# Retention's sample outputs in a decoder layer: the product of state and query columns moved from TensorE to ScalarE and VectorE, with TensorE summing one block a sample

## The chip, the cores and the metric

The kernel runs on one core of a Trainium2 chip. The metric is the device time of one execution in microseconds (us). Three executions were timed before the change; their median is 2566.97 us. The engines are named as in the profile: PE is TensorE (PEld its weight loads), DVE is VectorE, ACT is ScalarE, POOL is GpSimd, and SP is the engine whose queue issues nearly all transfers. Each of them works through its own list of instructions in order; an instruction that has to wait holds up all that stand behind it in its list.

## The reference

One decoder layer runs for two groups: a prompt of 16 + 256 tokens, and 8 samples that each have one new token and a state of earlier tokens. The layer is a feed-forward block, a mixer and a second feed-forward block. The mixer has two branches, and the change is in the retention branch: 8 heads with keys of 256 features and values of 256. For a sample it comes down to

```python
def retention_chunk(S, q, k, v):
    ...
    o = jnp.einsum('bhij,bhjv->bhiv', inner, v) + jnp.einsum('bhid,bhdv->bhiv', q_dec, S)
    ...
    S_new = jnp.exp(lg * C)[:, None, None].astype(S.dtype) * S + jnp.einsum('bhjd,bhjv->bhdv', k_dec, v)
    return S_new.astype(S.dtype), o
```

With one token a sample this is the same as: the new state is S_new = gamma * S + k v^T (256 x 256 a sample and head), and the output is o = S_new^T q, a row of 256. S_new is itself an output of the kernel (state_ret_sample), and o goes on through a normalisation, a gate and the output projection.

## The kernel before

Tokens stand in columns and features in the 128 partitions, so a vector of 256 features is two halves of 128 partitions each. All dense products (feed-forward blocks, the mixer's input projection, its output projection) are done by one loop, `dense` (L201 to L220): for each 128 x 128 block of weights there are three matmuls at L218, since a weight is split in two parts, `whi` and `wlo`, and so are the tokens (`xh`, `xl`). The weights come in units of eight blocks (512 KB). One unit takes these steps in `stream` (L170): a transfer into `raw` (L185, issued by SP), a copy to `whi` on ACT (L188), a subtraction that gives `wlo` on DVE (L189), and then 24 matmuls on PE. `raw`, `whi` and `wlo` have three buffers each. SP can issue the transfer of a unit only when DVE has made the `wlo` of the unit three before it, and ACT can make a `whi` only when PE has finished with the unit three before it.

The input projection (`project`) runs head after head, with the next head's columns in front of the previous head's gates. Between its steps of k, `pump` (L617) lets other work in: the mixers of the heads are generators (`mix_hg` for the other branch, `mix_ret` for retention), and `yield n` in them means that n pumps go by before the next piece is issued. On PE the order is as written; on the other engines the scheduler orders the work, and it gives the weight steps of `stream` high priority.

`mix_ret(u, q, k, v)` does retention for head u. What matters here of its sample part:

- Four tiles `sms[0]` to `sms[3]` (tag `smr`, four buffers that `ks` and `vs` use too) hold the states of the head: `sms[2 * e + c]` has half c of the key features for the four samples 4e to 4e + 3, as 128 partitions x 4 x 256.
- ACT scales a tile by gamma (L1192, four ACTIVATEs a head of 128 x 1024), and DVE adds key times value (L1198, sixteen instructions a head of 128 x 256, one for each sample and half). The result is the new state, in place.
- SP stores each tile to `out_srs` (L1202), four stores of 512 KB a head, here called S1 to S4: S1 and S2 are the halves 0 and 1 of e = 0, S3 and S4 those of e = 1.
- After more pumps, PE makes the outputs of the eight samples in the bank `pqr` (L1211): for each sample and half one matmul whose moving operand is the 128 x 256 state and whose stationary operand is 32 columns of `qdr`, a tile of zeros in which only the sample's own query column stands. So 16 matmuls a head go into four groups of 32 rows (`tile_position`), in which the sums run over halves and over e. `alone(qdr, q)` (L1133, helper L733) puts the query's columns in place on DVE, once a head.
- ACT copies `pqr` out (L1217), and `sample_columns` (L738) later turns the rows into columns of the head's output.

These matmuls only read the tiles, and a store only reads them too, so before the change neither waits for the other.

Of the kernel before, what the change touches and what calls it, by code (L numbers as in the profile page):

```python
# [13 lines left out]
AF = mybir.ActivationFunctionType  # L14
ALU = mybir.AluOpType
# [3 lines left out]
P = 128  # L19
# [4 lines left out]
NMETA, SEQ, NS = 16, 256, 8  # L24
# [27 lines left out]
ALONE = 4 * 32 + 1  # L52
# [76 lines left out]
def trunk(ctx: ExitStack, tc: tile.TileContext, A, O):  # L129
    nc = tc.nc  # L130
# [12 lines left out]
    def mx_bank(name):  # L143
        return ps_m.tile([P, 512], F32, tag="mx", name=name)
# [94 lines left out]
    def mul(out, a, b):  # L239
        nc.vector.tensor_tensor(out=out, in0=a, in1=b, op=ALU.mult)  # L240
# [306 lines left out]
    with tc.tile_pool(name="yp", bufs=1) as yp:  # L547
# [7 lines left out]
        with tc.tile_pool(name="mp", bufs=1) as mp:  # L555
# [7 lines left out]
            def tmp(name, shape=(P, T), bufs=1, dt=F32, tag=None):  # L563
                if name in rows:
                    rows[name] = rows[name][1:] + rows[name][:1]
                    return rp.tile(list(shape), dt, tag=rows[name][-1], name=name)
                return mp.tile(list(shape), dt, tag=tag or name, name=name, bufs=bufs)
# [19 lines left out]


            qdh = tmp("qdh", (P, 4, ALONE))
            qdr = tmp("qdr", (P, 4, ALONE))  # L590
            nc.gpsimd.memset(qdh, 0.0)
            nc.gpsimd.memset(qdr, 0.0)
            qdh_at = [qdh.rearrange("p a c -> p (a c)")[:, 256 * h :] for h in range(2)]
            qdr_at = [qdr.rearrange("p a c -> p (a c)")[:, 2 * ALONE * c :] for c in range(2)]
            vsm = tmp("vsm", (P, P))
            vt2 = tmp("vt2", (P, 2, P))
            scr2 = tmp("scr2", (P, NMETA))
# [50 lines left out]
            def evacuate(n, c0, c1, o0, o1, b0, b1):  # L648
# [33 lines left out]
                elif n == "v_r":  # L682
                    v = tmp("v", (P, 2, T))
                    nc.scalar.copy(v[:, 0, :], o0)
                    nc.scalar.copy(v[:, 1, :], o1)
                    start(mix_ret(c0 // 2, st["q_r"], st["k_r"], v), 24 if c0 == 2 else 3)
                elif n in ("g_r", "g_h"):
                    sg = tmp("gs", (P, TL), bufs=2)
                    t = tmp("gt", (P, TL), bufs=2)
                    nc.scalar.activation(sg, o0, AF.Sigmoid)  # L690
                    mul(t, sg, o0)
                    sa = tmp("gs", (P, TL), bufs=2)
                    nc.scalar.activation(sa, o1, AF.Sigmoid)
                    mul(t, t, sa)
                    u, e = divmod(c0, 2)
                    while u not in (done_r if n == "g_r" else done_h):
                        pump()
                    if n == "g_r":
                        y = tmp("y", (P, TL))
                        mul(y, t, on_r[u][:, e, :])  # L700
                        st["y"] = y
                    else:
                        y = st["y"]
                        nc.vector.scalar_tensor_tensor(
                            out=t, in0=t, scalar=ngt[:, c0 : c0 + 1], in1=on_h[u][:, e, :], op0=ALU.mult, op1=ALU.mult)

                        ys[c0] = y if c0 < EARLY else yp.tile([P, TL], F32, tag=f"y{c0}", name=f"y{c0}")
                        add(ys[c0], y, t)
                        if c0 < EARLY:
                            split(yh[c0], yl[c0], y)  # L710
# [22 lines left out]
            def alone(qd, q):  # L733
                nc.vector.tensor_copy(
                    qd[:, :, : 128 : 32].rearrange("p (c e) j -> p c e j", e=2),
                    q[:, :, SEQ:].rearrange("p c (e j) -> p c e j", e=2))
# [348 lines left out]
            def mix_ret(u, q, k, v):  # L1085
# [3 lines left out]
                calm = 2  # L1089
                sms = []  # L1090
# [13 lines left out]
                for c in range(2):  # L1104
# [22 lines left out]
                    for x, g, his, i, lo in todo:  # L1127
                        for hi in his:
                            nc.scalar.activation(hi, x, AF.Copy, scale=g)
                        nc.vector.scalar_tensor_tensor(  # L1130
                            out=lo, in0=x, scalar=g, in1=his[i].bitcast(F32), op0=ALU.mult, op1=ALU.subtract)
                    yield 2
                alone(qdr, q)  # L1133
                vts = [vt[:, 0], vt[:, 1], vs2]
                vrow = rows_out(vt2.rearrange("p c f -> p (c f)")[16:24, :], 256, "vr")

# [25 lines left out]
                for c in range(2):  # L1162
# [9 lines left out]
                    if c == 0:  # L1172
                        gams = [tmp("gam", (P, 1))]
                        nc.gpsimd.tensor_scalar(
                            out=gams[0], in0=so[:, 0:1], scalar1=GAMMA[u], scalar2=GAMMA[u], op0=ALU.min, op1=ALU.max)
# [13 lines left out]
                for e in range(2):  # L1189
# [3 lines left out]
                    for i in (2 * e, 2 * e + 1):  # L1193
                        for c in range(2):
                            for b in (2 * i, 2 * i + 1):
                                x, t = ss[c][:, b - 4 * e, :], LP + b
                                kk = late_k[:, c, b - 4 : b - 3] if e else k[:, c, t : t + 1]
                                nc.vector.scalar_tensor_tensor(  # L1198
                                    out=x, in0=vbs[i][:, b - 2 * i, :], scalar=kk, in1=x, op0=ALU.mult, op1=ALU.add)
# [1 line left out]
                    for c in range(2):  # L1201
                        nc.sync.dma_start(O["srs"][u, c, :, 4 * e : 4 * e + 4, :], ss[c])  # L1202
                    yield 1 if e else 10 if u == 0 else 6
                yield (11 if u == 0 else 15) + 2 * calm
                pq = mx_bank("pqr")
                scores(pq[:, 256:], 2)
                for e in range(2):
                    for c in range(2):
                        for j in range(4):
                            b = 4 * e + j  # L1210
                            nc.tensor.matmul(  # L1211
                                pq[32 * j : 32 * j + 32, :256], qdr_at[c][:, 32 * b : 32 * b + 32],
                                sms[2 * e + c][:, j, :], start=e + c == 0, stop=e + c == 2, tile_position=(0, 32 * j))
                mul(scr2[:NB2], pq[:NB2, 256 : 256 + NMETA], dt[:NB2, c2:])
                upper_upper_lower(sc2, scr2[:NB2])
                os = tmp("osr", (P, 256))
# [160 lines left out]
```

## Time and profile before

| | |
| --- | --- |
| time, median of 3 (lowest to highest) | 2566.97 us (2566.27 to 2568.13) |
| span of the profiled execution, first to last instruction | 2563.9 us |
| stretch in which `pqr` matmuls run (8 heads) | 859.8 to 1698.6 us |
| transfers of the core over the span | 536.26 MB, mean 209 GB/s |

The profile gives a span for the profiled execution, and no time of its own beside it; the median stands 3.07 us above that span, and this is taken for what lies around it. In the tables below, a row of a timeline has the start in us, the duration in us (of the whole row where several instructions are merged), the engine, the line, the operation, `out<-in` with the program's names, and the count; a bracket behind it tells how long the engine sat idle before it and what ended that. A row of a group has the count, then busy us and mean ns of one, then idle us before and what ended it. Matmuls in fp32 show as two records each, so the 16 matmuls of a head are 32 records. "SPq" is SP's queue of transfers, and the times in its rows are those of the issue, not of the transfer.

### The profile page before, as it was taken

How to read it: one execution, taken by the hardware profiler on the slowest of the kernel's cores; microseconds unless marked ns; L12 is line 12 of the kernel's file. 1: busy time of each engine (PE TensorE's matmuls, PEld its weight loads, DVE VectorE, ACT ScalarE, POOL GpSimd, SP SyncE). 2: the span in 40 equal slices, each digit the busy share in tenths (PEclk: the TensorE clock that was granted, in tenths of full speed). 3: DMA queues.
4: the chain of work that ended last, by engine and by line, in shares of the span. 5: the costliest groups of instructions: out<-in, count | busy, mean ns of one | idle time of the engine just before them, and what ended most of it. 6: DMA issues, size and time to landing. Idle time of an engine off the chain costs nothing.

```text
span 2563.9 us, 56275 instructions
## 1 busy us (share of the span) xinstructions
PE 2553.4 (100%) x23424; PEld 2534.4 (99%) x23424; DVE 1702.8 (66%) x2827; ACT 1392.2 (54%) x2186; POOL 57.0 (2%) x152
## 2 busy tenths in 40 slices
PE   9999999999999999999999999999999999999999
PEld 9999999999999999999999999999999999999998
DVE  6444544475569878777777777777885555556555
ACT  5444444444456767767676666675564444444443
POOL 0000000000000000000000000000000000000000
PEclk9999999999999999999999999999999999999999
DMA  7555555555555876767676767675556565565554
GB/s 244 183 187 183 187 182 184 186 182 186 184 201 180 287 265 232 264 214 260 212 264 215 259 223 255 224 239 188 196 190 197 194 197 195 194 196 195 195 195 149
DMA packets 156897, 536.26 MB, mean 209 GB/s; under 512 B 17952, under 2 KB 25952, under 8 KB 156640
## 3 DMA queue, kind: packets, MB, share of 16 engines
q1 hardware_dynamic: 156352, 532.37, 62.0%
q8 instruction: 183, 3.00, 0.5%
q14 instruction: 74, 0.61, 0.1%
q10 hardware_dynamic: 288, 0.29, 0.0%
HBM read 501.99 MB, written 30.61 MB: 208 GB/s over the span
## 4 chain that ended last, share of the span: by engine, by line
PE 96%; DVE 2%; ACT 0%; issue 0%; DMA 0%; SPq 0%; ACTq 0%; DVEq 0%
PE up L218 36%; PE dn L218 19%; PE pj_i_h L218 3%; PE pj_g_r L218 3%; PE pj_q_h L218 3%; PE pj_g_h L218 3%; PE pj_a_r L218 3%; PE pj_a_h L218 3%; PE pj_f L218 3%; PE pj_q_r L218 3%; PE pj_k_r L218 3%; PE wo L218 3%; PE pj_v_r L218 3%; DVE wlo L189 1%; PE pqr L1211 1%; PE psr L1168 0%
## 5 line engine op out<-in xcount | busy, mean ns | idle before, releaser
L189 DVE TENSOR_TENSOR wlo<-raw,whi 128x1024 fp32r<-128x1024 f32 (+1 forms) x869 | 1062.2, 1223 | 740.7 <-ACT whi L188 737.3
L188 ACT CAST whi<-raw 128x1024 fp32r<-128x1024 f32 (+1 forms) x870 | 905.7, 1042 | 909.2 <-PE up L218 411.0
L218 PE MATMUL up<-xh,whi 128*128 128x280 f32 (+1 forms) x2624 | 725.6, 280 | 0.6 <-ACT whi L188 0.6
L218 PE MATMUL up<-xh,wlo 128*128 128x280 f32 (+1 forms) x2624 | 725.8, 280 | 0.4 <-DVE wlo L189 0.3
L218 PE MATMUL up<-xl,whi 128*128 128x280 f32 (+1 forms) x2624 | 725.4, 279 | 0.0
L218 PEld LDWEIGHTS up<-xh,wlo 128*128 128x128 f32 x2624 | 492.6, 189 | 1.0 <-DVE wlo L189 1.0
L218 PEld LDWEIGHTS up<-xh,whi 128*128 128x128 f32 x2624 | 492.6, 189 | 0.8 <-ACT whi L188 0.8
L218 PEld LDWEIGHTS up<-xl,whi 128*128 128x128 f32 x2624 | 492.6, 189 | 0.0
L218 PE MATMUL dn<-hh,whi 128*128 128x280 f32 (+1 forms) x1376 | 384.7, 280 | 0.0
L218 PE MATMUL dn<-hh,wlo 128*128 128x280 f32 (+1 forms) x1376 | 384.3, 279 | 0.0
L218 PE MATMUL dn<-hl,whi 128*128 128x280 f32 (+1 forms) x1376 | 384.3, 279 | 0.0
L218 PEld LDWEIGHTS dn<-hh,whi 128*128 128x128 f32 x1376 | 260.1, 189 | 0.1
L218 PEld LDWEIGHTS dn<-hl,whi 128*128 128x128 f32 x1376 | 260.1, 189 | 0.1
L218 PEld LDWEIGHTS dn<-hh,wlo 128*128 128x128 f32 x1376 | 260.1, 189 | 0.0
L218 PE MATMUL pj_k_r<-xh,whi 128*128 128x280 f32 x256 | 74.2, 290 | 0.0
L218 PE MATMUL pj_g_r<-xh,whi 128*128 128x264 f32 x256 | 74.0, 289 | 0.0
L218 PE MATMUL pj_v_r<-xh,whi 128*128 128x280 f32 x256 | 73.8, 288 | 0.0
L218 PE MATMUL pj_v_r<-xh,wlo 128*128 128x280 f32 x256 | 72.4, 283 | 0.3 <-DVE wlo L189 0.3
L218 PE MATMUL pj_g_h<-xh,whi 128*128 128x264 f32 x256 | 72.7, 284 | 0.0
L218 PE MATMUL pj_k_r<-xh,wlo 128*128 128x280 f32 x256 | 72.4, 283 | 0.0
L218 PE MATMUL pj_v_r<-xl,whi 128*128 128x280 f32 x256 | 72.3, 283 | 0.0
L218 PE MATMUL pj_k_r<-xl,whi 128*128 128x280 f32 x256 | 72.3, 283 | 0.0
(421 smaller groups left out, 5263.4 us busy)
## 6 DMA issues: line engine op xcount, KB each, us to landing
raw<-in_w_up SPq DMA_DIRECT2D x343, 512.0 KB, 4.1
raw<-in_w_in SPq DMA_DIRECT2D x320, 512.0 KB, 4.3
raw<-in_w_dn SPq DMA_DIRECT2D x172, 512.0 KB, 3.5
smr<-in_sr SPq DMA_DIRECT2D x32, 512.0 KB, 5.0
out_srs<-smr SPq DMA_DIRECT2D x32, 512.0 KB, 6.7
raw<-in_w_out SPq DMA_DIRECT2D x32, 512.0 KB, 3.9
vbr<-vrd SPq DMA_DIRECT2D x32, 256.0 KB, 4.1
smh<-in_sg SPq DMA_DIRECT2D x16, 512.0 KB, 5.2
```

Source lines behind the costliest of these rows:

```text
L188: nc.scalar.copy(hi[:, j:jn, :], raw[:, j:jn, :])
L189: nc.vector.tensor_tensor(out=lo[:, j0:j1, :], in0=raw[:, j0:j1, :], in1=hi[:, j0:j1, :].bitcast(F32), op=ALU.subtract)
L218: nc.tensor.matmul(o, w, t, start=start, stop=stop)
L1211: nc.tensor.matmul(pq[32 * j : 32 * j + 32, :256], qdr_at[c][:, 32 * b : 32 * b + 32], sms[2 * e + c][:, j, :], start=e + c == 0, stop=e + ...
```

## The change

The product of state and query column leaves PE. A new tile `one` takes the place of `qdr`: zeros with a column of ones at the sample's place, set once for all heads. After the new state has been made and its stores have been issued, ACT multiplies half 0 of each sample's state by the query column's half 0, in place (eight ACTIVATEs of 128 x 256 a head), and DVE multiplies half 1 by the query's half 1 and adds what ACT made, in place (eight instructions of 128 x 256). PE then only has to sum over the 128 partitions: one matmul a sample with the ones, 8 a head where there were 16. `alone(qdr, q)` goes away. The single `yield` ahead of the matmuls is cut into pieces with the same sum, so that the two parts of four samples are issued some pumps ahead.

```diff
             qdh = tmp("qdh", (P, 4, ALONE))
-            qdr = tmp("qdr", (P, 4, ALONE))
+            one = tmp("one", (P, 2, ALONE))
             nc.gpsimd.memset(qdh, 0.0)
-            nc.gpsimd.memset(qdr, 0.0)
+            nc.gpsimd.memset(one, 0.0)
+            nc.gpsimd.memset(one[:, :, : 128 : 32], 1.0)
...
-                alone(qdr, q)
...
                     for c in range(2):
                         nc.sync.dma_start(O["srs"][u, c, :, 4 * e : 4 * e + 4, :], ss[c])
                     yield 1 if e else 10 if u == 0 else 6
-                yield (11 if u == 0 else 15) + 2 * calm
+                yield 4 if u == 0 else 8
+                for e in range(2):
+                    s0, s1 = sms[2 * e : 2 * e + 2]
+                    for j in range(4):
+                        t = SEQ + 4 * e + j
+                        nc.scalar.activation(s0[:, j, :], s0[:, j, :], AF.Copy, scale=q[:, 0, t : t + 1])
+                        nc.vector.scalar_tensor_tensor(
+                            out=s1[:, j, :], in0=s1[:, j, :], scalar=q[:, 1, t : t + 1], in1=s0[:, j, :], op0=ALU.mult, op1=ALU.add)
+                    yield 4
+                yield (11 if u == 0 else 15) + 2 * calm - 8 - (4 if u == 0 else 8)
                 pq = mx_bank("pqr")
                 scores(pq[:, 256:], 2)
                 for e in range(2):
-                    for c in range(2):
-                        for j in range(4):
-                            b = 4 * e + j
-                            nc.tensor.matmul(
-                                pq[32 * j : 32 * j + 32, :256], qdr_at[c][:, 32 * b : 32 * b + 32],
-                                sms[2 * e + c][:, j, :], start=e + c == 0, stop=e + c == 2, tile_position=(0, 32 * j))
+                    for j in range(4):
+                        b = 4 * e + j
+                        nc.tensor.matmul(
+                            pq[32 * j : 32 * j + 32, :256], one_at[:, 32 * b : 32 * b + 32],
+                            sms[2 * e + 1][:, j, :], start=e == 0, stop=e == 1, tile_position=(0, 32 * j))
```

PE's list of instructions is the same as before but for these matmuls; they stand at the same place. On ACT, DVE and SP the scheduler's order shifts. The lists around the outputs of head u = 3 show it, in the rows of the step that puts the new work in and of those that wait for it; heads 4 to 7 look the same, heads 0 to 2 nearly so. A bracket gives the semaphores for which an instruction waits: of another engine, or of a transfer (`DMAHW0` to `DMAHW7`, which SP's transfers take in turn, each transfer the next one).

On ACT, around the outputs of head 3, before the change (five weight units, `whi`, whose transfers ended with the semaphores 7, 2, 4, 6 and 7):

```order
L188 CAST whi_15246<-raw_15245 128x8x128 [waits DMAHW7_49,DVE_49,PE_49]
L690 ACTIVATE gs<-pj_g_h_15035 128x264 [waits PE_49]
L188 CAST whi_15276<-raw_15275 128x8x128 [waits DMAHW2_49,DVE_49,PE_49]
L693 ACTIVATE gs<-pj_a_h_15036 128x264 [waits PE_49]
L188 CAST whi_15354<-raw_15353 128x8x128 [waits DMAHW4_49,DVE_49,PE_49]
L188 CAST whi_15395<-raw_15394 128x8x128 [waits DMAHW6_49,DVE_49,PE_49]
```

and now:

```order
L188 CAST whi_15283<-raw_15282 128x8x128 [waits DMAHW7_49,DVE_49,PE_49]
L1209 ACTIVATE smr<-smr,q_r 128x256 [waits DMAHW3_49]
L1209 ACTIVATE smr<-smr,q_r 128x256
L188 CAST whi_15313<-raw_15312 128x8x128 [waits DMAHW2_49,DVE_49,PE_49]
L1209 ACTIVATE smr<-smr,q_r 128x256 x2
L691 ACTIVATE gs<-pj_g_h_15056 128x264
L694 ACTIVATE gs<-pj_a_h_15057 128x264 [waits PE_49]
L188 CAST whi_15383<-raw_15382 128x8x128 [waits DMAHW4_49,DVE_49,PE_49]
L1209 ACTIVATE smr<-smr,q_r 128x256 [waits DMAHW7_49,DVE_49]
L188 CAST whi_15424<-raw_15423 128x8x128 [waits DMAHW6_49,DVE_49,PE_49]
```

Two of the new ACTIVATEs now stand ahead of the second `whi`, and one ahead of the fourth. The first of each group waits for a transfer's semaphore: the one after the weights' 2, which is S1's (3), and the one after the weights' 6, which is S3's (7).

On DVE, at the same place, before:

```order
L189 TENSOR_TENSOR wlo_15277<-raw_15275,whi_15276 128x8x128 [waits DMAHW2_49,PE_49,Activation_49]
L240 TENSOR_TENSOR gt<-gt,gs 128x264 [waits DVE_49,Activation_49]
L704 SCALAR_TENSOR_TENSOR gt<-gt,ngt,on_h 128x264 [waits DVE_49]
L252 TENSOR_TENSOR y_15211<-y,gt 128x264 [waits DVE_49]
L189 TENSOR_TENSOR wlo_15355<-raw_15353,whi_15354 128x8x128 [waits DMAHW4_49,PE_49,Activation_49]
L189 TENSOR_TENSOR wlo_15396<-raw_15394,whi_15395 128x8x128 [waits DMAHW6_49,PE_49,Activation_49]
L240 TENSOR_TENSOR scr_8637<-pqr,dtab 16x16 [waits PE_49]
```

and now:

```order
L189 TENSOR_TENSOR wlo_15314<-raw_15312,whi_15313 128x8x128 [waits DMAHW2_49,PE_49,Activation_49]
L240 TENSOR_TENSOR gt<-gs,pj_g_h_15056 128x264 [waits Activation_49]
L1210 SCALAR_TENSOR_TENSOR smr<-smr,q_r 128x256 [waits DMAHW5_49]
L1210 SCALAR_TENSOR_TENSOR smr<-smr,q_r 128x256 x2
L189 TENSOR_TENSOR wlo_15384<-raw_15382,whi_15383 128x8x128 [waits DMAHW4_49,PE_49,Activation_49]
L1210 SCALAR_TENSOR_TENSOR smr<-smr,q_r 128x256
L240 TENSOR_TENSOR gt<-gt,gs 128x264 [waits DVE_49]
L705 SCALAR_TENSOR_TENSOR gt<-gt,ngt,on_h 128x264 [waits DVE_49]
L252 TENSOR_TENSOR y_15240<-y,gt 128x264 [waits DVE_49]
L189 TENSOR_TENSOR wlo_15425<-raw_15423,whi_15424 128x8x128 [waits DMAHW6_49,PE_49,Activation_49]
L1210 SCALAR_TENSOR_TENSOR smr<-smr,q_r 128x256 [waits DMAHW2_49]
L1210 SCALAR_TENSOR_TENSOR smr<-smr,q_r 128x256 [waits Activation_49] x3
```

Three of the new DVE instructions stand between the second and the third `wlo`, one behind the third, and the last four behind the fourth, right ahead of the work that waits for PE's outputs. The first of e = 0 waits for semaphore 5 (S2's), the first of e = 1 for semaphore 2.

On SP, the transfers of the same stretch as they stand now (raw_15312, raw_15382, raw_15423, raw_15492 and raw_15522 are weight units, `out_srs` the stores S1 to S4):

```order
L185 DMA raw_15312<-in_w_in 128x1024 [waits DMAHW2_49,DVE_49]
L1202 DMA out_srs<-smr 128x1024 [waits DMAHW3_49]
L185 DMA raw_15382<-in_w_in 128x1024 [waits DMAHW4_49,DVE_49]
L1202 DMA out_srs<-smr 128x1024 [waits DMAHW5_49]
L185 DMA raw_15423<-in_w_in 128x1024 [waits DMAHW7_49,DMAHW6_49,DVE_49]
L1202 DMA out_srs<-smr 128x1024 [waits DVE_49]
L185 DMA raw_15492<-in_w_in 128x1024 [waits DMAHW2_49,DMAHW0_49,DVE_49]
L185 DMA raw_15522<-in_w_in 128x1024 [waits DMAHW4_49,DMAHW1_49,DVE_49]
L1202 DMA out_srs<-smr 128x1024
```

Before, S3 stood one weight unit later, between the units that are now raw_15492 and raw_15522; S1, S2 and S4 stand where they stood. Counted on from the 6 of raw_15423, S3 takes 7, the two weight units 0 and 1, and S4 takes 2, so the semaphore 2 for which DVE waits ahead of its last four is that of S4.

On PE, the eight matmuls on `one` now wait for DVE:

```order
L1040 MATMUL pq<-smh,qdh 32x128 x7
L1141 MATMUL pqr<-q_r,k_r 16x16 x2
L1219 MATMUL pqr<-smr,one 32x256 [waits DVE_49] x8
L218 MATMUL pj_g_r_15242<-xh_11_9280,whi_15313 128x264
L218 MATMUL pj_g_r_15242<-xl_11_9281,whi_15313 128x264
```

There were 16 on `qdr` at this place, and none of them waited for DVE.

More of the change, by code (lines that the diff above doesn't have):

```diff
@@ L589, in trunk @@
             qdh = tmp("qdh", (P, 4, ALONE))
-            qdr = tmp("qdr", (P, 4, ALONE))
+            one = tmp("one", (P, 2, ALONE))
             nc.gpsimd.memset(qdh, 0.0)
-            nc.gpsimd.memset(qdr, 0.0)
+            nc.gpsimd.memset(one, 0.0)
+            nc.gpsimd.memset(one[:, :, : 128 : 32], 1.0)
             qdh_at = [qdh.rearrange("p a c -> p (a c)")[:, 256 * h :] for h in range(2)]
-            qdr_at = [qdr.rearrange("p a c -> p (a c)")[:, 2 * ALONE * c :] for c in range(2)]
+            one_at = one.rearrange("p a c -> p (a c)")
             vsm = tmp("vsm", (P, P))
```

## The prediction, made before the changed kernel had run

> **What bounds the kernel now.** First the head of the page and its chain of waits, then the list of what PE waited for.
>
> ```profile
> span 2563.9 us, 56275 instructions
> ...
> PE 2553.4 (100%) x23424; PEld 2534.4 (99%) x23424; DVE 1702.8 (66%) x2827; ACT 1392.2 (54%) x2186; POOL 57.0 (2%) x152
> ...
> PE 96%; DVE 2%; ACT 0%; issue 0%; DMA 0%; SPq 0%; ACTq 0%; DVEq 0%
> ```
>
> PE is busy over the whole span and makes up 96% of the chain that ended last. The reader is to see two things. An instruction taken off PE is worth its full time; and everything that makes PE wait, on whatever engine it lies, is paid in full as well. In this profile PE waits for practically nothing: the longest rows of its waits are these two (columns: what waited, for whom, the sum in us, how often, the longest).
>
> ```profile
> PE pw L515 <- DVE eps_h L163: 1.0, 1, 1.0
> PE pt L1116 <- POOL tails L1103: 0.9, 1, 0.9
> ```
>
> **What goes from PE.** The group of the sample outputs, and its timeline in head 3:
>
> ```profile
> L1211 PE MATMUL pqr<-smr,qdr 128*32 128x256 f32 x256 | 15.5, 381 | 0.0
> ```
>
> ```profile
> 1191.60 0.42 PE L1211 MATMUL pqr<-smr,qdr 128*32 128x256 f32 x3
> ...
> 1191.65 1.89 PE L1211 MATMUL pqr<-smr,qdr 128*32 128x256 f32 x29
> ...
> 1193.47 0.38 PE L218 MATMUL pj_g_r<-xh,whi 128*128 128x264 f32 x1
> ```
>
> The last row's 0.38 us is one matmul's way through the array; the records themselves follow each other every (1.89 - 0.38) / 28 = 0.054 us. The change takes 16 of the 32 records a head: 8 x 16 x 0.054 = **6.9 us** off PE, 0.27% of the span. That is all that the change can win, since PE's list is otherwise the same, in the same order.
>
> **What comes to ACT and DVE.** Eight ACTIVATEs and eight DVE instructions of 128 x 256 a head. DVE's kind is in the trace; ACT's isn't, and lies between two rows that are.
>
> ```profile
> L1198 DVE SCALAR_TENSOR_TENSOR smr<-vbr,sro,smr 128x256 f32<-128x256 f32 x64 | 27.5, 478 | 1.9 <-DMA vbr<-vrd 1.8
> ...
> L1192 ACT ACTIVATE smr<-smr,sro 128x1024 f32<-128x1024 f32 x16 | 18.2, 1147 | 7.5 <-DMA smr<-in_sr 7.4
> ...
> L998 ACT ACTIVATE smh<-smh,meta 128x128 f32<-128x128 f32 x128 | 41.1, 391 | 0.4
> ```
>
> From 391 ns (128 columns) and 1147 ns (1024 columns) an ACTIVATE of 256 columns comes to 391 + 128 x 756 / 896 = about 500 ns, less in a row: some 0.40 us. DVE's take 0.48 alone and 0.40 each in a row (three of them in 1.27 in a row below). So each engine gets 3.2 to 4 us a head, and DVE loses the little copying of `alone`. By itself this hides behind PE: ACT is busy for 54% and DVE for 66%. If that cover were gone for the pieces next to the matmuls, 8 x 4 = 32 us would be the price; it is not what I count on, for the wait below covers them.
>
> **The wait that is added.** The products are written in place, over tiles that SP's stores S1 to S4 still read. So the order's brackets show L1209 and L1210 waiting for semaphores of those very stores, which rise when the transfer has landed. Before, nothing waited for them before the next head. How late that is stands in the row on line 1202 (issue to landing, all 32) and in SP's timeline of head 3:
>
> ```profile
> DMA to landing us min/median/max: 6.4/6.7/7.3
> ```
>
> ```profile
> 1179.92 0.33 SPq L185 DMA_DIRECT2D raw<-in_w_in  x1
> 1180.31 0.42 SPq L1202 DMA_DIRECT2D out_srs<-smr  x1
> 1182.72 0.33 SPq L185 DMA_DIRECT2D raw<-in_w_in  x1
> 1183.11 0.50 SPq L1202 DMA_DIRECT2D out_srs<-smr  x1
> ...
> 1188.89 0.43 SPq L1202 DMA_DIRECT2D out_srs<-smr  x1
> ...
> 1191.35 0.33 SPq L185 DMA_DIRECT2D raw<-in_w_in  x1
> 1191.73 0.49 SPq L1202 DMA_DIRECT2D out_srs<-smr  x1
> ```
>
> S4 is issued at 1191.73, and PE wants the outputs at 1191.60. With the change PE waits until S4 has landed and DVE has made the four products behind it: 6.7 + 3 x 0.40 + 0.48 = 6.7 + 1.7 us. And S4 itself goes later, through DVE's queue:
>
> ```profile
> 1185.73 1.27 DVE L1198 SCALAR_TENSOR_TENSOR smr<-vbr,sro,smr 128x256 f32<-128x256 f32 x3
> ...
> 1187.26 1.22 DVE L189 TENSOR_TENSOR wlo<-raw,whi 128x1024 fp32r<-128x1024 f32 x1
> ...
> 1190.10 1.23 DVE L189 TENSOR_TENSOR wlo<-raw,whi 128x1024 fp32r<-128x1024 f32 x1 [0.29 <-ACT whi L188]
> ```
>
> ```profile
> 1185.35 1.05 ACT L188 CAST whi<-raw 128x1024 fp32r<-128x1024 f32 x1 [1.97 <-DMA raw<-in_w_in]
> ```
>
> S1 lands at 1180.31 + 6.7 = 1187.0. ACT, in its list, does two products first (1187.8) and then the `whi` that stood at 1185.35 (1188.85), behind which the `wlo` of 1187.26 ends at 1190.1. S2 lands at 1189.8, before that. A gate product (taken as 0.4) and three products on DVE end at 1191.8, and only then comes the `wlo` of 1190.10, some 1.8 late. SP's weight transfer of 1191.35 waits for that `wlo` to give a buffer back, and S4 stands behind it in SP's queue: issued at 1193.5 instead of 1191.73. It lands at 1200.2, the products end at 1201.9, and PE, ready at 1191.6, waits **10.3 us**. What it finds then is enough to go on: 12 matmuls of a unit and two units more are ready, against some 3.5 us for the next `whi` and `wlo`.
>
> For the other heads the same sum, (issue of S4 - start of `pqr`) + delay of S4 + 6.7 + 1.7, with these rows:
>
> ```profile
> 856.47 1.06 SPq L1202 DMA_DIRECT2D out_srs<-smr  x1
> ...
> 859.77 0.42 PE L1211 MATMUL pqr<-smr,qdr 128*32 128x256 f32 x3
> ...
> 947.58 0.50 SPq L1202 DMA_DIRECT2D out_srs<-smr  x1
> ...
> 950.22 0.42 PE L1211 MATMUL pqr<-smr,qdr 128*32 128x256 f32 x3
> ...
> 1064.75 0.57 SPq L1202 DMA_DIRECT2D out_srs<-smr  x1
> ...
> 1065.27 0.42 PE L1211 MATMUL pqr<-smr,qdr 128*32 128x256 f32 x3
> ...
> 1317.73 1.35 SPq L1202 DMA_DIRECT2D out_srs<-smr  x1
> ...
> 1317.94 0.42 PE L1211 MATMUL pqr<-smr,qdr 128*32 128x256 f32 x3
> ...
> 1697.01 0.42 PE L1211 MATMUL pqr<-smr,qdr 128*32 128x256 f32 x3
> ...
> 1697.41 1.50 SPq L1202 DMA_DIRECT2D out_srs<-smr  x1
> ```
>
> Heads 0 to 2 have a little more room, and the walk through their lists delays S4 by 3.4, 3.0 and 1.9. Head 0: -3.3 + 3.4 + 6.7 + 1.7, and 1.1 for a `wlo` that stands between its last products: 9.6. Head 1: -2.64 + 3.0 + 8.4 = 8.8. Head 2: -0.52 + 1.9 + 8.4 = 9.8. Heads 3 to 7 have S4 within -0.55 to +0.40 of `pqr` (the first and last of them are above) and the delay of head 3: 10.3, 10.0, 9.9, 9.7, 10.6. Together **79 us**. The bounds of the landing: the shortest transfer that touches these tiles, loads included, takes 4.2, the longest 8.7; I take the stores' own 6.7.
>
> ```profile
> DMA to landing us min/median/max: 4.2/6.6/8.7
> ```
>
> **What a stall does to PE's clock.** PE never pauses in this trace but at its two ends. At the start, its first matmuls (128 x 128) run beside others of that shape in mid-kernel like this:
>
> ```profile
> 1.05 4.55 PE L515 MATMUL pw<-ones 128*128 128x128 f32 x22 [1.05 <-DVE eps_h L163]
> ```
>
> ```profile
> 885.08 0.22 PE po L1050 x2
> ```
>
> At the end, the stretch without matmuls shows a granted clock of 0.69 (columns: us, PE, PEld, DVE, ACT and POOL busy with counts, PEclk, DMA share, GB/s):
>
> ```profile
> 2557.00:2560.00 3.00, 0.89 (x4) 0.40 (x3) 3.00 (x9) 2.94 (x6) 0.00 (x0) 1.00 0.87 297
> 2560.00:2564.00 4.00, 0.00 (x0) 0.00 (x0) 0.01 (x1) 0.65 (x2) 0.00 (x0) 0.69 0.60 203
> ```
>
> The last matmul ended at 2557.89. If the clock is halved when it falls, 0.69 over 4 us means half for 2.5 us, so it fell at about 2561.5, 3.6 us behind that matmul; a stall of 9 to 10 us is well over that. Coming back from idle costs what the start cost: 22 matmuls in 4.55 instead of 22 x 0.11 = 2.4, so 2.1 us a stall, **17 us** for eight. This is an estimate: nothing excludes 0 on one side, or the whole 4.55 a stall (36 us) on the other; I take the row that shows the effect.
>
> [...]
>
> **The sum.** 2563.9 (span) + 79 + 17 - 6.9 = 2653 for the profiled execution, and 3.1 around it: **2656 us**. The execution before stands at 2567.0 in the same way, which is the median of the runs shown.
>
> **Rivals.** (1) The stalls come, but the clock doesn't fall, or recovers without a cost: 2656 - 17 = 2639. For it: the page's clock row shows full clock in the first 4 us, where the matmuls were slow, so the two needn't be one thing.
>
> (2) The stores land sooner: with PE stopped, its weights are not fetched, and the transfers have the engines to themselves. At 4.2 instead of 6.7 the stall loses 2.5 a head, and S1 and S2 have landed before ACT and DVE come to them, so the delays (3.4 + 3.0 + 1.9 + 5 x 1.8 = 17) go too: 79 - 20 - 17 = 42. With 12 for the clock, these stalls being shorter, 2563.9 + 42 + 12 - 6.9 + 3.1 = 2614. Against it: S1 and S2 are issued while PE is still running.
>
> (3) After the stall the weights are late as well. DVE has stood still for 7 us, and SP's next transfers behind it. If PE then lacks one unit a head, which is worth the 2.8 us between the weight transfers of 1179.92 and 1182.72, it costs 8 x 2.8 = 22: 2678. Against it: two units are ready.
>
> (4) The other side: the semaphores that L1209 and L1210 wait for are reached by older transfers of the same number, and no store holds the products up. Then DVE's last state at 1187.0 (1185.73 + 1.27) and about 4 us of products end at 1191, ahead of 1191.6; PE never waits and the time is 2567 - 7 = 2560. It decides whether the last four products can end by 1191.6, so S4 would have to land by 1189.9, before it is even issued; hence only an order in which the wait isn't for S4 can give this. The order's count of the numbers speaks against it: S4 takes 2, and the last four wait for 2.
>
> That the change doesn't do what it says is ruled out by PE's list: 8 matmuls a head for 16.
>
> **How the numbers follow.** My forecast has 0.54, rival 1 0.15, rival 2 0.13, rival 3 0.12, rival 4 0.06. Range 2610 to 2685: the low end takes in rival 2, the high one rival 3 or the dearer clock (2656 + 19 = 2675), with 2 x 0.6 x 8 = 10 more if the landings are at their longest, 7.3. What stays outside is rival 4 and stalls longer or shorter than all of these. About 0.2%, 5 us, is what a measurement of this kernel can tell from no change. Only rival 4 is on the faster side: faster 0.04, within 0.2% 0.02, slower 0.94.
>
> **What would show it.** Right: eight gaps in PE's row ahead of line 1219, each some 9 to 10 us, ended by DVE line 1210, which itself waits for a transfer `out_srs`; PE's group at line 1219 with 128 records in place of 256; SP's S4 some 2 us later against `pqr` than before; matmuls behind each gap at double their spacing for some 4 us, and a granted clock under 1 in these slices. Wrong: no gaps, or gaps ended by ACT's `whi` (then it is the weights, rival 3), or by DVE without a transfer behind it (then the products themselves are too slow); full spacing right behind a gap (rival 1); landings near 4 us (rival 2).

## The result, and the profile after

| | before | with the change |
| --- | --- | --- |
| time, median of 4 (lowest to highest) | 2566.86 us (2566.27 to 2568.13) | 2642.26 us (2637.56 to 2644.39) |
| span of the profiled execution | 2563.9 us | 2642.4 us |

The change makes the kernel slower by 2.9%: the ratio is 1.0291, 95% interval 1.0277 to 1.0304. The forecast was 2656 us, in a range from 2610 to 2685.

The head of the page, with the chain that ended last:

```profile
span 2642.4 us, 56139 instructions
...
PE 2579.2 (98%) x23296; PEld 2546.9 (96%) x23296; DVE 1729.4 (65%) x2883; ACT 1416.8 (54%) x2250; POOL 54.0 (2%) x153
...
PE 87%; DMA 5%; DVE 5%; ACT 2%; issue 1%; SPq 0%; ACTq 0%; DVEq 0%
PE up L218 34%; PE dn L218 18%; DMA out_srs<-smr 4%; PE pj_v_r L218 3%; PE pj_q_h L218 3%; PE pj_f L218 3%; PE pj_k_r L218 3%; PE wo L218 3%; PE pj_q_r L218 3%; PE pj_i_h L218 3%; PE pj_g_r L218 2%; DVE wlo L189 2%; PE pj_a_r L218 2%; PE pj_g_h L218 2%; PE pj_a_h L218 2%
```

PE has 128 records less, and its share of the chain has fallen from 96% to 87%. A store of state, `out_srs`, was on no chain before and now holds 4% of it. The reader should not be misled by PE's busy time, which rose by 26 us though it has less to do: the outputs' own matmuls, spread out by the wait, are busy for 25.5 us in place of 15.5, and a matmul at half clock is busy for longer (0.43 us in place of 0.28 for those of L218 below).

The waits (who waited for whom, us in all, times, longest):

```profile
PE pqr L1219 <- DVE smr L1210: 43.1, 10, 6.6
...
ACT smr L1209 <- DMA out_srs<-smr: 42.7, 13, 6.2
...
DVE smr L1210 <- DMA out_srs<-smr: 24.5, 11, 3.8
```

These three rows are the chain store, product, PE. The timelines of SP, ACT, DVE and PE around the outputs of head 3 show it link by link (start in us, duration, engine, line, operation, `out<-in`, count, and in the bracket the idle time ahead and what ended it):

```profile
1207.55 0.42 SPq L1202 DMA_DIRECT2D out_srs<-smr  x1
1209.02 0.33 SPq L185 DMA_DIRECT2D raw<-in_w_in  x1
1209.41 2.36 SPq L1202 DMA_DIRECT2D out_srs<-smr  x1
...
1217.98 3.00 SPq L185 DMA_DIRECT2D raw<-in_w_in  x2
1221.03 0.43 SPq L1202 DMA_DIRECT2D out_srs<-smr  x1
```

```profile
1214.85 0.91 ACT L1209 ACTIVATE smr<-smr,q_r 128x256 f32<-128x256 f32 x2 [5.95 <-DMA out_srs<-smr]
1215.67 1.03 ACT L188 CAST whi<-raw 128x1024 fp32r<-128x1024 f32 x1
```

```profile
1218.21 1.27 DVE L1210 SCALAR_TENSOR_TENSOR smr<-smr,q_r 128x256 f32<-128x256 f32 x3
1219.40 1.22 DVE L189 TENSOR_TENSOR wlo<-raw,whi 128x1024 fp32r<-128x1024 f32 x1
...
1227.32 1.67 DVE L1210 SCALAR_TENSOR_TENSOR smr<-smr,q_r 128x256 f32<-128x256 f32 x4 [3.83 <-DMA out_srs<-smr]
```

```profile
1221.01 0.68 PE L1219 MATMUL pqr<-smr,one 128*32 128x256 f32 x6
1227.87 2.25 PE L1219 MATMUL pqr<-smr,one 128*32 128x256 f32 x8 [6.17 <-DVE smr L1210]
1230.04 0.59 PE L218 MATMUL pj_g_r<-xh,whi 128*128 128x264 f32 x1
1230.43 0.43 PE L218 MATMUL pj_g_r<-xl,whi 128*128 128x264 f32 x1
1230.65 0.43 PE L218 MATMUL pj_g_r<-xh,wlo 128*128 128x264 f32 x1
```

ACT stands for 5.95 us until S1 has landed, 7.3 us after its issue at 1207.55, with a `whi` behind it. SP's weight transfers of 1217.98 wait for buffers, and S4 behind them goes out at 1221.03, just when PE comes to the outputs. PE does the matmuls of e = 0 and then stands: DVE starts the last four products at 1227.32, when S4 has landed, 6.3 us after its issue. When PE goes on, the matmuls at 1230.43 and 1230.65 follow each other at 0.22 us, where this kernel's pace is 0.11.

The clock over the same stretch (columns: us, busy and counts of PE, PEld, DVE, ACT and POOL, then the granted clock, DMA share, GB/s):

```profile
1221.00:1226.00 5.00, 0.69 (x16) 0.21 (x11) 2.42 (x5) 1.82 (x5) 0.00 (x0) 1.00 0.85 261
1226.00:1228.00 2.00, 0.14 (x1) 0.14 (x2) 0.68 (x2) 0.00 (x0) 0.00 (x0) 0.51 0.82 250
1228.00:1230.00 2.00, 2.00 (x8) 0.58 (x7) 1.00 (x3) 0.00 (x0) 0.00 (x0) 0.50 0.88 293
1230.00:1232.00 2.00, 2.00 (x10) 1.96 (x10) 1.05 (x5) 1.18 (x4) 0.00 (x0) 0.50 0.35 141
1232.00:1234.00 2.00, 2.00 (x16) 2.00 (x16) 1.50 (x2) 0.64 (x1) 0.00 (x0) 0.78 0.00 0
```

It fell to one half at 1226.0, 4.3 us after PE's last matmul had ended (1221.69), and was back at 1232.9, since a mean of 0.78 over 2 us is half for 0.9 us.

To see where the 78.5 us of span went, each matmul of PE is set beside the same one of before, and the growth of the difference is read in three parts, summed over the eight heads: **15.3 us** ahead of the outputs (mostly PE's waits for late weights: its rows for `whi` and `wlo` of the projection sum to 9.5 us, and in head 4 the clock also stood at half for 3.4 us ahead of the outputs, from 1355.8 to 1359.2), **53.1 us** from the first matmul on the states to the next weight matmul (14.9 us before, 68.0 now), and **10.1 us** in the 60 records behind it (half clock). Each head takes between 8.1 and 10.7 of the 78.5 us.

### The profile page after: what moved, and what is told of

Read it like the earlier page. It is cut to its first block, busy times and chain, and to the rows that moved or that the text cites. A ratio compares the mean times of both kernels' runs of the same rounds, so it can differ in the third digit from the quotient of the medians.

```text
span 2642.4 us, 56139 instructions
## 1 busy us (share of the span) xinstructions
PE 2579.2 (98%) x23296; PEld 2546.9 (96%) x23296; DVE 1729.4 (65%) x2883; ACT 1416.8 (54%) x2250; POOL 54.0 (2%) x153
## 4 chain that ended last, share of the span: by engine, by line
PE 87%; DMA 5%; DVE 5%; ACT 2%; issue 1%; SPq 0%; ACTq 0%; DVEq 0%
PE up L218 34%; PE dn L218 18%; DMA out_srs<-smr 4%; PE pj_v_r L218 3%; PE pj_q_h L218 3%; PE pj_f L218 3%; PE pj_k_r L218 3%; PE wo L218 3%; PE pj_q_r L218 3%; PE pj_i_h L218 3%; PE pj_g_r L218 2%; DVE wlo L189 2%; PE pj_a_r L218 2%; PE pj_g_h L218 2%; PE pj_a_h L218 2%
## 5 line engine op out<-in xcount | busy, mean ns | idle before, releaser
L218 PE MATMUL up<-xh,wlo 128*128 128x280 f32 (+1 forms) x2624 | 726.0, 280 | 0.5 <-DVE wlo L189 0.3
L218 PE MATMUL up<-xh,whi 128*128 128x280 f32 (+1 forms) x2624 | 725.7, 280 | 0.3 <-ACT whi L188 0.2
L218 PE MATMUL up<-xl,whi 128*128 128x280 f32 (+1 forms) x2624 | 725.4, 279 | 0.0
L218 PEld LDWEIGHTS up<-xh,wlo 128*128 128x128 f32 x2624 | 492.5, 189 | 1.3 <-DVE wlo L189 1.3
L218 PEld LDWEIGHTS up<-xh,whi 128*128 128x128 f32 x2624 | 492.6, 189 | 0.7 <-ACT whi L188 0.7
L218 PEld LDWEIGHTS up<-xl,whi 128*128 128x128 f32 x2624 | 492.6, 189 | 0.0
L218 PE MATMUL dn<-hh,whi 128*128 128x280 f32 (+1 forms) x1376 | 384.7, 280 | 0.0
L218 PE MATMUL dn<-hl,whi 128*128 128x280 f32 (+1 forms) x1376 | 384.3, 279 | 0.0
L218 PE MATMUL dn<-hh,wlo 128*128 128x280 f32 (+1 forms) x1376 | 384.3, 279 | 0.0
L218 PEld LDWEIGHTS dn<-hl,whi 128*128 128x128 f32 x1376 | 260.1, 189 | 0.1
L218 PEld LDWEIGHTS dn<-hh,whi 128*128 128x128 f32 x1376 | 260.1, 189 | 0.1
L218 PEld LDWEIGHTS dn<-hh,wlo 128*128 128x128 f32 x1376 | 260.1, 189 | 0.0
L218 PE MATMUL pj_g_r<-xh,whi 128*128 128x264 f32 x256 | 77.2, 302 | 1.7 <-ACT whi L188 1.7
L218 PE MATMUL pj_g_r<-xh,wlo 128*128 128x264 f32 x256 | 73.5, 287 | 4.2 <-DVE wlo L189 4.2
L218 PE MATMUL pj_k_r<-xh,whi 128*128 128x280 f32 x256 | 74.2, 290 | 0.0
L218 PE MATMUL pj_v_r<-xh,whi 128*128 128x280 f32 x256 | 73.8, 288 | 0.0
L218 PE MATMUL pj_g_h<-xh,whi 128*128 128x264 f32 x256 | 72.9, 285 | 0.3 <-ACT whi L188 0.3
L218 PE MATMUL pj_g_r<-xl,whi 128*128 128x264 f32 x256 | 72.9, 285 | 0.0
L218 PE MATMUL pj_g_h<-xh,wlo 128*128 128x264 f32 x256 | 71.0, 277 | 2.0 <-DVE wlo L189 2.0
L218 PE MATMUL pj_v_r<-xh,wlo 128*128 128x280 f32 x256 | 72.4, 283 | 0.3 <-DVE wlo L189 0.3
```

The source lines that it names most:

```text
L218: nc.tensor.matmul(o, w, t, start=start, stop=stop)
```

## Experiments

Theory A is that of the prediction: the products are written over tiles that the stores still read, so ACT, DVE and in the end PE wait for the stores to land. Rival B holds the added work on ACT and DVE responsible, whatever the stores do. Ratios are to the kernel before.

### e1: no stores

```diff
-                    for c in range(2):
-                        nc.sync.dma_start(O["srs"][u, c, :, 4 * e : 4 * e + 4, :], ss[c])
```

> Leaves out the four stores of the new state a head (state_ret_sample is not written); products in place and matmuls on the ones as in the change. Theory A (PE pays for stores that have to land before the products may be written over them): no wait is left at line 1219 and none of the weights ahead of it, so 2567 - 7 = 2560 us. Rival B (the work that came to ACT and DVE holds the weights up, whatever the stores do): the products are all still there, so most of the 75 us stays, 2620 us or more.

Measured: **2565.86 us**, ratio 0.9995 (0.9986 to 1.0005). All 75 us are gone with the stores, with all the new work still there, so B falls as the main cause. But the 6.9 us don't appear either. In head 3 DVE's last products and PE's matmuls now stand like this:

```profile
1193.22 0.88 DVE L1208 SCALAR_TENSOR_TENSOR smr<-smr,q_r 128x256 f32<-128x256 f32 x2
```

```profile
1192.96 0.42 PE L1217 MATMUL pqr<-smr,one 128*32 128x256 f32 x3
...
1193.01 1.77 PE L1217 MATMUL pqr<-smr,one 128*32 128x256 f32 x13
```

PE is at the outputs at 1192.96, and the last product ends at 1194.10. The matmuls come at the pace of DVE and take 1.77 us, almost the 1.89 of twice as many before. Over all heads the stretch shrinks by 1.6 us, not 6.9.

### e2: the products of e = 1 in tiles of their own

```diff
+                    if e:
+                        pr = [tmp("vbr", (P, 2, 256), bufs=2) for _ in range(2)]
...
-                        nc.scalar.activation(s0[:, j, :], s0[:, j, :], ...
+                        d1 = pr[j // 2][:, j % 2, :] if e else s1[:, j, :]
+                        d0 = d1 if e else s0[:, j, :]
+                        nc.scalar.activation(d0, s0[:, j, :], ...
...
```

and likewise for DVE's output and for what PE's matmuls read.

> All stores stay; only the products of e = 1 are written to tiles of their own (two vbr tiles, free at that time) and not over the state, so they don't wait for S3 and S4; those of e = 0 stay in place. Theory A: the stall at line 1219 and its half clock go; what is left are the weights' waits ahead of it, which e = 0 causes by waiting for S1 and S2 (about 1.5 us a head): 2560 + 12 = 2572 us. Rival B: 2642, nothing of the work has gone. If S1 and S2 were the stores that matter, also near 2642.

Measured: **2581.77 us**, 1.0058 (1.0043 to 1.0073). e1 also took the stores' transfers away; here nothing is left out. Only the place of half of the products differs, and 60 of the 75 us are gone. What PE still waits for are weights, since ACT and DVE stand at S1 and S2:

```profile
PE pj_g_r L218 <- DVE wlo L189: 3.8, 7, 0.8
PE pj_g_h L218 <- DVE wlo L189: 2.3, 3, 0.8
...
ACT smr L1213 <- DMA out_srs<-smr: 16.9, 8, 3.9
```

Set beside before in the same three parts, the losses are 14.0 us ahead of the outputs, 1.9 in them and none behind. So S3 and S4 own the stall and the half clock, and S1 and S2 the late weights ahead of it.

### e3: the outputs later

```diff
-                yield (11 if u == 0 else 15) + 2 * calm - 8 - (4 if u == 0 else 8)
+                yield (11 if u == 0 else 15) + 2 * calm - 8 - (4 if u == 0 else 8) + 16
```

> Products where the change has them, but PE's eight matmuls 16 pumps (16 x 0.68 = 10.9 us of PE's work) later. Theory A: S4 lands and its products end about 10 us after the old place, so PE no longer waits at line 1219; DVE and ACT still stand still for S3 and S4, and their weights come late by what three buffers (8 us) don't cover: 2565 to 2600 us. Rival B: 2642, as the work is the same.

Measured: **2595.32 us**, 1.0109 (1.0094 to 1.0124). PE's wait at line 1219 is gone, and 28 us more than before remain. Over all heads the stretch of the outputs takes 8.0 us here, where it took 14.9 before: where PE comes after the products, the whole 6.9 us are saved. The stores still hold ACT and DVE, who hold the weights:

```profile
PE pj_g_h L218 <- DVE wlo L189: 8.1, 10, 1.4
PE pj_g_r L218 <- DVE wlo L189: 4.5, 7, 0.8
...
ACT smr L1209 <- DMA out_srs<-smr: 45.5, 15, 6.6
DVE smr L1210 <- DMA out_srs<-smr: 26.1, 10, 4.3
```

### e4: work for PE inside the stall

```diff
                 scores(pq[:, 256:], 2)
+                for _ in range(16):
+                    nc.tensor.matmul(pq[:, 384:], ident, ident, start=True, stop=True)
```

> The change, with 16 added matmuls of 128 x 128 (32 records, 3.5 us) on constants between the scores and line 1219's matmuls, into an unused part of the bank. They run inside the stall. Theory A with the clock as read from the changed trace (half clock from some 4.7 us after PE stops until 5 us after it goes on): the idle time falls below that, the clock stays at 1, and 12 matmuls at 0.22 instead of 0.11 us and the last ones of line 1219 are won back, 1.3 to 1.7 us a head: 2642 - 12 = 2630 us. If the clock cost nothing, 2642; if the added matmuls were on the path, up to 2642 + 28 = 2670.

Measured: **2634.02 us**, 1.0259 (1.0244 to 1.0275). With 128 matmuls more it is 8.2 us faster than the change, so the half clock is real time. It won back less than was expected: in some heads the clock still fell, as in head 3 (mean 0.92 from 1221 to 1224), where PE had done the added matmuls by 1219.3 and stood again:

```profile
1219.00:1221.00 2.00, 0.87 (x11) 0.26 (x9) 0.00 (x0) 0.00 (x0) 0.00 (x0) 1.00 1.08 377
1221.00:1224.00 3.00, 1.27 (x7) 0.54 (x8) 1.67 (x4) 0.00 (x0) 0.00 (x0) 0.92 0.80 280
```

The losses behind the outputs went from 10.1 to 3.8 us.

### e5: the stores from POOL's queue

```diff
-                        nc.sync.dma_start(O["srs"][u, c, :, 4 * e : 4 * e + 4, :], ss[c])
+                        nc.gpsimd.dma_start(O["srs"][u, c, :, 4 * e : 4 * e + 4, :], ss[c])
```

> The change, but the four stores a head are issued by POOL's queue, where no weight transfer stands ahead of them. Products and matmuls stay. Theory A: S4 goes out when DVE has made the last state, some 4.4 us before the old issue (1187.3 against 1191.7 in head 3's old times) and 2 us more before the one of the change; landing at 6.4, products 1.7: PE waits about 4 us a head in place of 10, too short for the clock to fall: 2560 + 32 + some 8 for the weights = 2600 us. If the landing alone mattered and not the place in SP's queue: 2640.

Measured: **2610.91 us**, 1.0176 (1.0162 to 1.019). POOL issues S3 and S4 in head 3 right after the last state, not behind weights, and PE's wait shrinks from 43.1 to 17.7 us:

```profile
1207.14 0.53 POOL L1202 DMA_DIRECT2D out_srs<-smr  x1 [8.06 <-DVE smr L1198]
1207.94 0.53 POOL L1202 DMA_DIRECT2D out_srs<-smr  x1 [0.26 <-issue]
```

```profile
PE pqr L1219 <- DVE smr L1210: 17.7, 12, 5.0
```

So 31 us of the change's loss go when the stores take POOL's queue. Not all of this need be the place in SP's queue: the landings differ too (2.9 to 9.3 us with a median of 6.2 in e5's row, 5.7 to 6.7 with 6.4 in the change's). The time is near the expected 2600, but its parts are not: in the same three parts the losses are 17.3 us ahead of the outputs, 26.3 in them and 2.0 behind, where 8 and 32 were expected.

### e6: products and outputs later

```diff
-                yield 4 if u == 0 else 8
+                yield (4 if u == 0 else 8) + 16
...
-                yield (11 if u == 0 else 15) + 2 * calm - 8 - (4 if u == 0 else 8)
+                yield (11 if u == 0 else 15) + 2 * calm - 8 - (4 if u == 0 else 8) + 2
```

> Stores stay in SP's queue; the products are issued 16 pumps (10.9 us of PE) later and PE's eight matmuls 18 pumps later, so that the stores have landed when ACT and DVE come to the products. Theory A: no engine waits for a store any more, neither PE at line 1219 nor the weights behind ACT and DVE: between 2560 (all 16 records a head saved) and 2567 us. Rival B (the added work itself holds the weights up, or S_n's late landing only moves): over 2580.

Measured: **2607.53 us**, 1.0157 (1.0144 to 1.0171): a miss by 40 us, on the side where rival B was put. The waits for stores are not gone but longer than in the change:

```profile
ACT smr L1209 <- DMA out_srs<-smr: 55.7, 15, 6.4
DVE smr L1210 <- DMA out_srs<-smr: 28.8, 9, 5.0
```

The `yield` moves PE's matmuls, but ACT and DVE still come to the first products before S1 has landed and stand there for up to 6.4 us, with the weights behind them. Whether they are put there or only not held back is what e10 is for.

### e7: both

e5 with the products 6 and the matmuls 8 pumps later.

> Both: stores issued by POOL, products 6 pumps (4.1 us) later, matmuls 8 pumps (5.4 us) later. Theory A: S4 lands near 1194 in head 3's old times, its products end near 1196, PE comes at 1197: no wait, 2560 to 2567 us. If the transfers from POOL's queue land later than SP's, a rest of the stall stays: 2567 to 2600.

Measured: **2592.01 us**, 1.0099 (1.0085 to 1.0113), 19 us better than e5 alone. ACT still waits 29.5 us for stores, from POOL's queue with landings between 2.9 and 9.5 us:

```profile
ACT smr L1209 <- DMA out_srs<-smr: 29.5, 11, 6.0
```

```profile
DMA to landing us min/median/max: 2.9/6.0/9.5
```

### e8 and e9: all products in tiles of their own

The products of e = 0 go to the two `vbr` tiles, PE sums them, and those of e = 1 use the tiles again. So PE's matmuls come in two parts.

```diff
+                    pr = [tmp("vbr", (P, 2, 256), bufs=2) for _ in range(2)]
...
                     yield 4
...
+                    if e:
+                        yield 3
+                    else:
+                        pq = mx_bank("pqr")
+                        scores(pq[:, 256:], 2)
                     for j in range(4):
...
```

e9 has `yield 3 + 4`, and `yield 3` in place of the `yield 7` behind the outputs.

> All stores stay in SP's queue, at their places. All products go to vbr tiles (two tiles, used for e = 0 and again for e = 1), none over the state; so that the tiles come free, PE's four matmuls of e = 0 run four pumps after their products, those of e = 1 at the old place. Theory A: no engine waits for a store; as without the stores, 2560 to 2567 us. Rival B: 2580 or more, since all the work and all the transfers are there.

> As e8, with PE's matmuls of e = 1 four pumps (2.7 us) later, and four pumps less behind them. Without stores the last matmuls still ran at the pace of DVE's last products (0.4 us each) and the 6.9 us didn't show; if that is why, this gives 2560 us; if moving the outputs costs of itself (the losses behind line 1219 of the run with the outputs later), 2567 to 2575.

Measured: e8 **2591.11 us**, 1.0094 (1.0079 to 1.0109); e9 **2596.78 us**, 1.0116 (1.0101 to 1.0131). Both missed, and e8 lies where rival B was put. No engine waits for a store any more, but PE comes to the matmuls of e = 0 before DVE has made their products, and e9 hadn't moved these. The rows are e8's and e9's, of PE and its weight loads:

```profile
PEld pqr L1222 <- DVE vbr L1212: 22.3, 30, 3.4
PE pqr L1222 <- DVE vbr L1212: 13.2, 14, 3.3
```

```profile
PE pqr L1222 <- DVE vbr L1212: 14.4, 14, 3.3
```

### e10: products in place, held back

```diff
+                yield 12
+                qs = tmp("qs", (P, 2, NS))
+                pqq = mx_bank("pqq")
+                for c in range(2):
+                    nc.tensor.matmul(pqq[:, NS * c : NS * c + NS], ident, q[:, c, SEQ : SEQ + NS], start=True, stop=True)
+                nc.scalar.copy(qs.rearrange("p c b -> p (c b)"), pqq[:, : 2 * NS])
...
-                        nc.scalar.activation(s0[:, j, :], s0[:, j, :], AF.Copy, scale=q[:, 0, t : t + 1])
+                        nc.scalar.activation(s0[:, j, :], s0[:, j, :], AF.Copy, scale=qs[:, 0, t : t + 1])
...
```

and the same for DVE; PE's outputs are 16 pumps later than in the change.

> Products in place, stores in SP's queue. The query's columns go through PE (two matmuls with the identity) and ACT to a small tile, 12 pumps (8.2 us) later than the change issues the products, and the products take them from there, so ACT and DVE can't come to them earlier; PE's eight matmuls 16 pumps later. Tells apart why moving all later failed: if ACT and DVE stood at the stores because the products were still put ahead of the weights, their waits for stores go from 55.7 and 28.8 us to under 10 and only the losses behind line 1219 stay, some 22 us: 2580 to 2590. If the later place of the outputs was the whole cause, 2600 to 2610 as before.

Measured: **2579.95 us**, 1.0047 (1.003 to 1.0064). With the products tied to a later step of PE, the waits for stores are down to one row, and PE's wait for products is gone:

```profile
DVE smr L1216 <- DMA out_srs<-smr: 1.4, 3, 0.7
```

So the change's products can stay in place, and its stores in SP's queue, without a stall: it is their time that made it. In e6 it was ACT's and DVE's own order that kept them early. Of the 14 us by which this span exceeds that of before, 12.5 have come about by the end of the stretch behind head 1's outputs; heads 2 to 7 add 1.7 together, and from head 3 on the run loses nothing more (14.4 us behind before ahead of head 3's outputs, 14.2 at the end). In heads 0 and 1 PE waits for DVE at steps behind the outputs, and at one of the other branch (L1023):

```profile
PE pst L1023 <- DVE km L255: 2.2, 2, 1.7
PE por L1240 <- DVE sc L255: 1.5, 1, 1.5
PE por L742 <- DVE T L240: 1.5, 1, 1.5
PE por L742 <- DVE osr L1084: 1.1, 1, 1.1
```

These four rows sum to 6.3 of the 12.5 us. The mean granted clock of this run was 0.998, where the runs of before beside it had 0.999 to 1.000, so a part may have been lost there. What makes the rest, and why DVE is late, isn't settled.

### e11 and e12: all apart, with time for the products

As e8, with eight (nine) pumps ahead of the matmuls of e = 0 and six (eight) ahead of those of e = 1; `yield 4` (`yield 2`) behind the outputs. The diff is that of e11 against e8.

```diff
-                    yield 4
-                    if e:
-                        yield 3
-                    else:
+                    yield 6 if e else 8
+                    if not e:
...
-                yield 7
+                yield 4
```

> As e8 (all products in vbr tiles, stores where they are), but PE's matmuls of e = 0 eight pumps behind their products in place of four, and those of e = 1 three pumps later than in e8. In e8 no engine waited for a store, and what was lost were PE's waits at the matmuls of e = 0 for products that DVE had not yet made (some 3 us a head). Theory A, with that as e8's own fault: the waits go, 2560 to 2570 us. If in-place writing had hidden some other cost of the products (theory B in a smaller size), 2580 to 2590.

> The same with nine and eight pumps (six later than e8 in all). Theory A: as e11, or up to 5 us less where e11 still waits for DVE; if a later place of the outputs costs of itself, more than e11.

Measured: e11 **2576.69 us**, 1.004 (1.0027 to 1.0054); e12 **2589.95 us**, 1.0093 (1.0079 to 1.0106). In e11 PE's wait for products is nearly gone, and it is 14 us better than e8, though 10 us behind before: between the two ranges, so that some smaller cost of the added work isn't excluded. Of these 10 us 5.9 have come about by the end of head 1; what makes them isn't settled. In e12 the short `yield 2` has made a new wait, two steps further on:

```profile
PE pqr L1220 <- DVE vbr L1212: 0.9, 1, 0.9
```

```profile
PE por L742 <- DVE osr L1084: 8.8, 8, 1.3
PE por L1235 <- DVE sc L255: 8.4, 4, 6.2
```

None of these beats the kernel before. With the outputs at their old place there was little to win: even with no store at all (e1) the new way is worth 0.05%, within its interval. With the outputs later the 6.9 us are saved in their stretch (e3), but every such run lost more elsewhere; whether some order keeps them isn't shown.

## Why the prediction was right, and where its sizes were off

| step of the prediction | forecast | measured |
| --- | --- | --- |
| PE stalls and late weights, eight heads | 79 us | 75.3 (53.1 + 15.3 + 6.9 that the stretch would have shrunk by) |
| half clock behind the stalls | 17 us | 10.1, of which e4 won back 6.3 |
| saved on PE | 6.9 us | nothing to be seen; 1.6 without the stores (e1), 6.9 with PE later (e3) |
| span | 2653 us | 2642.4 |

- **What bounds the kernel, and that each wait of PE is paid in full:** right. The three parts add up to the whole 78.5 us.
- **The wait that is added:** right, and shown by e1 and e2. The chain of head 3 came nearly as written. The same matmuls would have come at 1191.60 + 27.3 (the lead that had gathered by then) = 1218.9; S4 was issued 2.1 us behind that (forecast 1.9), landed 6.3 us later (6.7), and the products took 1.67 (1.7). S1 took 7.3 us to land, not 6.7.
- **What the walk took for one stall is two.** The delay of S4, put at 17 us in all, shows ahead of the outputs, 15.3 us there, mostly as PE's own waits for weights, and not as a longer stop at the outputs. Also PE did the matmuls of e = 0 before it stopped, so only half were left behind the stall.
- **The clock:** it did fall to one half (0.50 in the stretch above), but the term was too large. The fall, read as 3.6 us behind PE's last matmul, came 2.2 us behind it in head 2 and 4.3 in head 3 (last section). 2.1 us a stall was read from the kernel's start; a stall cost 10.1 / 8 = 1.3 behind the outputs, as the first part of the slow time lies in the last matmuls of line 1219, which were waiting for DVE's products anyway (0.40 us each).
- **6.9 us saved:** this term didn't show in the change. The prediction held that the work on ACT and DVE hides behind PE by itself. The bulk of it does, but DVE's last products end when PE's matmuls run, so these take DVE's pace. e1 shows it without any store, and e3 that the size was right: with PE 16 pumps later the stretch is 6.9 us shorter.
- **Rivals.** No clock loss (2639) is near the time, but for another reason: the clock did fall. Shorter landings (2614): the row below has 5.7 to 6.7 us, and S1 of heads 3 and 4 took 7.3 and 7.5, so no. Weights late behind the stall: no, PE's waits for weights lie ahead of it. No wait at all: no.

```profile
DMA to landing us min/median/max: 5.7/6.4/6.7
```

- **How this row is read:** it takes in only the stores whose landing the trace holds, 6 of 32 here. In the row of before, which the prediction took for all 32, they are 10 (6.4 to 7.3 us).

## What to carry to other kernels

Before a result is worked on in place, ask who still reads the tile: a store in flight is a reader until it lands, in head 3 6.3 (S4) and 7.3 us (S1) after its issue, and its issue can stand behind other transfers of its queue. The price of a wait is not only its length: here it held the weights that stood behind it on ACT and DVE (15.3 us ahead of the outputs), and PE came out of it at half clock (10.1 us behind them). And a piece of work that is hidden on average still sets the pace where its last part is the one that is waited for: in e1 half the matmuls took 1.77 us, and all of them 1.89 before.

## What the runs showed of the hardware

In head 3 the clock fell 4.3 us after PE's last matmul. In head 2, PE's last matmul ended at 1083.90, and the mean over the next 4.3 us is 0.76:

```profile
1083.90:1088.20 4.30, 0.00 (x1) 0.00 (x0) 2.20 (x4) 2.51 (x6) 0.00 (x0) 0.76 0.83 270
```

That is half clock for 4.3 x 0.24 / 0.5 = 2.1 us of them, so here it fell 2.2 us after the matmul. Why the two heads differ isn't shown. In e4's head 3 PE stood for 2.9 us, and the mean clock was 0.92 from 1221 to 1224.

Over the whole span the mean granted clock was 0.988 with the change and 1.000 before. With the change it stood at one half in nine stretches around the outputs, 58.0 us in all.

Landings from SP's queue weren't all alike: S1 took 7.3 us in head 3 (issued at 1207.55, ACT goes on at 1214.85) and 7.5 in head 4 (1344.49 to 1352.03), more than the row's 6.7. From POOL's queue in e7 the row has 2.9 to 9.5 us, with a median of 6.0.
